# From a router's scores to its first expert: the first block's gather ahead of the extra blocks', accumulators cleared behind the sigmoid, filling products on TensorE

## The chip, the cores and the metric

The kernel runs on one core of a Trainium2 chip. The metric is the device time of one execution in microseconds (us); less is better. A core has five engines that run side by side, each in the order of its own instruction stream: TensorE (PE, matrix products and transposes; PEld is its loading of the stationary operand), VectorE (DVE), ScalarE (ACT), GpSimd (POOL) and SyncE (SP). Here SP issues nearly all weight transfers. POOL issues the transfers that fetch or add rows by index (indirect DMA), and also copies and broadcasts over partitions. They meet through semaphores: an instruction starts when all that it waits for has been signalled.

## What is computed

Two layers of a network over 256 latent and 256 context tokens of 1024 numbers. In each layer a mixer (attention and a linear recurrence) is followed by a mixture of experts, and the change lies between these two, in layer 0 alone, where both kinds of tokens pass through the experts. The router, cut to what matters:

```
scores = sigmoid(h @ router_w)                # 16 experts in 4 groups of 4
biased = scores + router_b
# the group with the largest sum of its two best wins; in it the two best experts
top_w  = scores of the two / their sum
for e in range(16):
    hid = silu(h @ w_gate[e]) * (h @ w_up[e])
    out = out + combine[:, e:e+1] * (hid @ w_down[e])   # combine: top_w, zero if not chosen
x  = x  + g2  * out[latent];  xc = xc + cg2 * out[context]
```

Everything is float32. A token is computed only for the two experts that it chose.

## The kernel before, in words

**Ahead of the router.** Layer 0 ends its mixer in tiles of 128 tokens, four of them. For the last step of each tile and each half h of its columns, `out_turn` (L1134) turns the tile's rows by four transposes (tile names pxa, xaT), and `out_logits` multiplies them with the router's matrix (plog); VectorE then forms the logits lg. `warm(x, n)` puts n products on PE whose result nobody reads; in a float32 product PE's trace has two records for each.

**`route` (L1274).** ScalarE clears two accumulators in PSUM, ccg and ccd (four instructions, L1286 and L1287, by a scale of zero over a constant), which the extra blocks below will use, and takes the sigmoid sc of the logits. In layer 1 there are no such clears, and ten fillers `warm(sc, 10)` stand here. VectorE adds the bias (bi) and finds the winning group and the chosen experts (A, Ab), the normed weights (mb), and PE counts by triangular products the rank of each token in its expert (prank, with Ab as one operand); rk holds it on VectorE. At the end the weight is split into three bfloat16 parts, columns 2 to 4 of `vals` (columns 0 and 1 hold a token's number).

**Slots.** Each expert of layer 0 has one main block of 64 slots and up to three extra blocks of 32; which of these are run is decided on the device by the count (a branch on each engine concerned, `extras`, L1555). `onehot(e)` (L1368) compares the ranks with a row of numbers: four VectorE instructions, one per token tile, each of 512 columns, 128 for each block, into one buffer that all experts share. `infos(e)` (L1378) multiplies it on PE with `vals` (pslot: 16 products of 5 columns, four for each of the four blocks), copies the result (sf), and VectorE gives for each slot the row to fetch (sgs), whether it is of a latent or a context token (sic), and the weight (sw). `gathers(e)` fetches the rows on POOL (xg for the main block, xgx for extra ones); three sets of buffers. `r["counts"]` (L1356) turns the counts into integers for the branches.

**An expert.** `xtranses` turns the rows (pxg to xgT, pxx to xxT); `up_stage` multiplies with the gate and up matrices: `up0` is eight steps of k, each a gate and an up product of 512 columns (a pair, 16 products in all), and `upx` the same for an extra block (32 rows, 256 columns, into ccg). `hid0` and `hidx` form silu(gate) times up (hid, hix; ACT, then DVE). `htranses` and `down_stage` follow (pdn, and ccd for extra blocks). `pick0` and `pickx` choose for each slot the gate g2 or cg2 of the residual, `weigh` multiplies result, weight and gate, and `scatter` adds the rows to the layer's output (yd) by indirect DMA. All matrix products are issued through one helper, so in the profile they share the line L114; they are told apart by their tiles.

`gates2` (L1472) prepares the two gates on POOL, once: four broadcasts of a row over the partitions, each with three copies, and then two subtractions (g2m, g2x) which take the second gate less the first.

**What sets the order.** The whole expert stage is in a manual schedule: PE, POOL, DVE and ACT run exactly in the order in which the Python code is written (from L1630). SP's weight transfers (L216) go to a ring of eight chunks of 2 MB; each waits until the products that read the chunk's former content are done, and from expert 4's on also for an activation of the expert (`mark`), so that the queue stays short. Where written order matters most:

```
onehot(0); infos(0); warm(ident, 8); counts; gathers(0); wd_1 on POOL's queue
onehot(1); infos(1); gathers(1); loads of expert 2
onehot(2); xtranses(0); infos(2); gathers(2); gates2(); onehot(3)
up_stage(0)
infos(3); xtranses(1); gathers(3); onehot(4); htranses(0); up_stage(1); infos(4)
e = 0: down_stage(0); pick0, pickx; weigh, scatter; xtranses(2); gathers(4); onehot(5); infos(5); ...
```

Of the kernel before, what the change touches and what calls it, by code (L numbers as in the profile page):

```python
# [108 lines left out]
def backbone(ctx: ExitStack, tc: tile.TileContext, a: dict):  # L109
# [28 lines left out]
    def ps_tr(name):  # L138
        return psb(name, "tr")
# [326 lines left out]
    def mixer(l, R, hp, hT, mo):  # L466
# [667 lines left out]
        def out_turn(h, t):  # L1134
            pt = ps_tr("pxa")
            for k in range(4):
                pe.transpose(pt[:, k * P:(k + 1) * P], xa[t, h][:, k * P:(k + 1) * P], ident)
            xa[t, h, 1] = hc = t2("xaT")
            act.copy(hc[:], pt)
            if h:  # L1140
                finish(t)
# [132 lines left out]
    def route(l, lg, Q, R):  # L1274
# [8 lines left out]
        cps = {}  # L1283
        for n_ in () if last else ("cg", "cd"):
            t = pp["pool"].tile([P, 1024], F32, name=f"c{n_}", tag=n_, bufs=1)
            act.activation(t[:, 0:512], C("iota"), AF.Copy, scale=0.0)  # L1286
            act.activation(t[:, 512:768], C("iota")[:, 0:256], AF.Copy, scale=0.0)  # L1287
            cps[n_] = t[:, 0:768].rearrange("p (b c) -> p b c", b=3)
        bk.update(cps=cps)
        if last:  # L1290
            warm(sc[:].rearrange("p t e -> p (t e)"), 10)
# [57 lines left out]
        w1 = Q.tile(E16, F32, name="w1")  # L1349
        dve.tensor_copy(vals[:, 0:nt, :, 2], wc[:])  # L1350
        dve.tensor_tensor(w1[:], wc[:], vals[:, 0:nt, :, 2], op=OP.subtract)
        dve.tensor_copy(vals[:, 0:nt, :, 3], w1[:])
        dve.tensor_tensor(w1[:], w1[:], vals[:, 0:nt, :, 3], op=OP.subtract)
        dve.tensor_copy(vals[:, 0:nt, :, 4], w1[:])
# [45 lines left out]

    bk = {}
# [11 lines left out]
    def experts(l, tmp):  # L1413
# [31 lines left out]
        def up0(ps, x, w):  # L1445
            for k in range(8):
                sx = x[:, k % 4, 64 * (k // 4):64 * (k // 4) + 64]
                mm(ps[0:64, :], sx, w[0][:, k, :], k == 0, k == 7)
                mm(ps[64:128, :], sx, w[1][:, k, :], k == 0, k == 7)
# [180 lines left out]
        with tc.manual_schedule(engines=ORDERED):  # L1630
            W[1] = [load_part(l, 1, 0, nc.sync), wx["w"][0][0]]
            wx["i"] += 1
            onehot(0)
            infos(0)
            warm(ident, 8)
            r["counts"](tmp)
            gathers(0)
            W[1].append(load_part(l, 1, 2, nc.gpsimd))
            onehot(1)
            infos(1)  # L1640
            gathers(1)
            W[2] = [load_part(l, 2, i, nc.gpsimd if i < 2 else nc.sync) for i in range(3)]
            onehot(2)
            xtranses(0)
# [4 lines left out]
            up_stage(0)  # L1649
# [375 lines left out]
```

## Time and profile before

| | |
|---|---|
| median of 3 runs | 1109.69 us (1105.55 to 1113.52) |
| the profiled execution, its own time | 1107.49 us |
| its span in the trace | 1105.6 us |
| PE busy | 984.8 us, 89% |
| DVE, ACT, POOL busy | 600.5 (54%), 432.3 (39%), 195.7 (18%) |
| products of expert weights, layer 0 (pdn and both pgu<-..xgT) | 124.3, 118.7, 118.7 us, mean of one 617 to 619 ns |
| HBM traffic | 271 GB/s over the span |

The time of the whole is that of the profiled execution; the span is the trace's own, from its first to its last instruction, 1.9 us less. All places below are times from the span's start. In a row of the timeline stand start, busy time, engine, line, operation, tile written <- tiles read, shape, how many instructions the row gathers, and in brackets how long the engine was idle before and what ended that. The granted clock in a window is 1.00 for 2.4 GHz and 0.50 for 1.2 GHz. In a share of busy time PE's products overlap, so a product's mean is longer than the step from one to the next.

### The profile page before, as it was taken

How to read it: one execution, taken by the hardware profiler on the slowest of the kernel's cores; microseconds unless marked ns; L12 is line 12 of the kernel's file. 1: busy time of each engine (PE TensorE's matmuls, PEld its weight loads, DVE VectorE, ACT ScalarE, POOL GpSimd, SP SyncE). 2: the span in 40 equal slices, each digit the busy share in tenths (PEclk: the TensorE clock that was granted, in tenths of full speed). 3: DMA queues.
4: the chain of work that ended last, by engine and by line, in shares of the span. 5: the costliest groups of instructions: out<-in, count | busy, mean ns of one | idle time of the engine just before them, and what ended most of it. 6: DMA issues, size and time to landing. Idle time of an engine off the chain costs nothing. (4 is left out here: it accounts for less than half of the span.)

```text
span 1105.6 us, 15540 instructions
## 1 busy us (share of the span) xinstructions
PE 984.8 (89%) x5791; PEld 520.2 (47%) x5791; DVE 600.5 (54%) x1363; ACT 432.3 (39%) x858; POOL 195.7 (18%) x208
## 2 busy tenths in 40 slices
PE   5999999899589989999898599897977999999993
PEld 3555465678444434333332366353765434444431
DVE  3567487686743325534433356679863344444445
ACT  3635678465511212212221264796741122221222
POOL 2000033331544313212110200205241000000000
PEclk9999999899669989999998799998997999999996
DMA  9947674011866876999997565558156799999941
GB/s 381 396 167 299 229 272 186 30 39 58 323 244 259 286 287 190 398 407 410 395 397 305 155 268 188 200 180 305 49 210 270 317 421 413 429 400 416 397 197 41
DMA packets 51963, 298.87 MB, mean 270 GB/s; under 512 B 5457, under 2 KB 8401, under 8 KB 35969
## 3 DMA queue, kind: packets, MB, share of 16 engines
q1 hardware_dynamic: 44800, 279.88, 64.1%
q0 software_dynamic: 6896, 16.87, 5.4%
q8 instruction: 73, 1.20, 0.4%
q10 hardware_dynamic: 144, 0.52, 0.1%
q14 instruction: 50, 0.40, 0.1%
HBM read 288.86 MB, written 10.49 MB: 271 GB/s over the span
## 5 line engine op out<-in xcount | busy, mean ns | idle before, releaser
L114 PE MATMUL pdn<-wd,hidT 128*64 128x512 f32 x512 | 124.3, 619 | 5.3 <-PEq L1572 4.0
L114 PE MATMUL pgu<-wg,xgT 128*64 128x512 f32 x256 | 118.7, 617 | 0.3 <-issue 0.3
L114 PE MATMUL pgu<-wu,xgT 128*64 128x512 f32 x256 | 118.7, 617 | 0.2 <-DMA wu<-exp_w_up_dram 0.2
L114 PE MATMUL pgu<-wu,xT 128*64 128x512 f32 x256 | 116.5, 598 | 0.0
L114 PE MATMUL pgu<-wg,xT 128*64 128x512 f32 x256 | 116.5, 598 | 0.0
L1795 DVE SCALAR_TENSOR_TENSOR xtok<-pcb,wc,xtok 128x512 f32<-128x512 f32 x64 | 47.7, 750 | 102.7 <-PE pcb L114 102.7
L1455 DVE TENSOR_TENSOR hid<-hid,pgu 64x512 f32<-64x512 f32 x16 | 11.0, 690 | 126.2 <-ACT hid L1454 126.2
L114 PE MATMUL pproj<-hh,wps 128*128 128x512 f32 x288 | 76.9, 407 | 0.0
L846 POOL TENSOR_TENSOR wo<-wf,wo 128x512 fp32r<-128x512 f32 x29 | 41.0, 1434 | 201.9 <-ACT wo L844 170.1
L1430 POOL DMA_INDIRECT yd<-xtok,sgs x24 | 38.6, 1608 | 185.0 <-DVE xtok L1489 183.5
L114 PEld LDWEIGHTS pdn<-wd,hidT 128*64 128x64 f32 x512 | 34.7, 140 | 67.5 <-issue 66.8
L114 PEld LDWEIGHTS pgu<-wg,xgT 128*64 128x64 f32 x256 | 34.8, 142 | 65.2 <-issue 64.7
L114 PEld LDWEIGHTS pproj<-hh,wps 128*128 128x128 f32 x288 | 53.2, 188 | 19.6 <-issue 6.5
L114 PEld LDWEIGHTS pgu<-wg,xT 128*64 128x64 f32 x256 | 32.5, 136 | 61.6 <-issue 60.7
L1454 ACT ACTIVATE hid<-pgu 64x512 f32<-64x512 f32 x16 | 9.4, 590 | 104.8 <-PE pgu L114 104.7
L1954 POOL TENSOR_TENSOR fin<-xtok,fin 128x512 f32<-128x512 f32 x2 | 2.5, 1278 | 254.8 <-DVE xtok L1795 254.8
L1748 ACT ACTIVATE hid<-pgu 64x512 f32<-64x512 f32 x16 | 9.4, 589 | 94.6 <-PE pgu L114 94.5
L795 ACT ACTIVATE Pm<-psc,mx,qy 128x512 f32<-128x512 f32 (+1 forms) x48 | 33.5, 703 | 21.3 <-DVE mx L789 21.1
L497 DVE TENSOR_TENSOR wps<-win,wps 128x512 fp32r<-128x512 f32 x48 | 32.6, 687 | 14.9 <-ACT wps L496 14.4
L114 PE MATMUL pproj<-hT,wps 128*128 128x512 f32 x144 | 39.8, 397 | 0.0
L114 PEld LDWEIGHTS pgu<-wu,xgT 128*64 128x64 f32 x256 | 34.8, 142 | 6.9 <-issue 5.2
L114 PE MATMUL pwa<-wo,mh 128*128 128x512 f32 x128 | 36.3, 407 | 1.6 <-POOL wo L846 0.9
(442 smaller groups left out, 2079.5 us busy)
## 6 DMA issues: line engine op xcount, KB each, us to landing
wd<-exp_w_down_dram SPq DMA_DIRECT2D x31, 2048.0 KB, 14.2
wu<-exp_w_up_dram SPq DMA_DIRECT2D x27, 2048.0 KB, 9.6
wg<-exp_w_gate_dram SPq DMA_DIRECT2D x27, 2048.0 KB, 15.9
xtok<-ada_w_dram SPq DMA_DIRECT2D x7, 2048.0 KB, 7.4
win<-w_in_dram SPq DMA_DIRECT2D x6, 2048.0 KB, 16.2
adac<-ada_w_dram SPq DMA_DIRECT2D x5, 2048.0 KB, 8.0
xtok<-ada_w_dram SPq DMA_DIRECT2D x8, 1024.0 KB, 5.1
adac<-ada_w_dram SPq DMA_DIRECT2D x8, 1024.0 KB, 4.9
```

Source lines behind the costliest of these rows:

```text
L114: pe.matmul(out, lhsT, rhs, start=start, stop=stop)
L497: dve.tensor_tensor(wl, wv, wh.bitcast(F32), op=OP.subtract)
L795: act.activation(ps[h], sc_[i][h], AF.Exp, bias=mx[:, h:h + 1], scale=qr[:, ti, j, h:h + 1], accum_out=sm[:, h:h + 1])
L846: pool.tensor_tensor(lo, w, hi.bitcast(F32), op=OP.subtract)
L1430: st = pool.indirect_dma_start(out=dst, out_offset=bass.IndirectOffsetOnAxis(ap=idx, axis=0), in_=y, in_offset=None, bounds_check=dst.shap ...
L1454: mark.append(act.activation(sg, ps[0:64, :], AF.Silu).ins.name)
L1455: dve.tensor_tensor(h.rearrange("s k p -> s (k p)"), sg, ps[64:128, :], op=OP.mult)
L1748: act.activation(sg, ps[0:64, :], AF.Silu)
L1795: dve.scalar_tensor_tensor(x, cb, wc[:, t, e:e + 1], x, op0=OP.mult, op1=OP.add)
L1954: (dve if q else pool).tensor_tensor(fin["t"][:, 1 + t, cs], x, fin["t"][:, 0, cs], op=OP.mult)
```

## The change: what it does

All of it is in layer 0. (a) `out_turn` puts seven fillers ahead of each half of the last tile's transposes. (b) In `route` the sigmoid comes first; the clears read the sigmoid (times zero) and so stand behind it on ScalarE. Twenty fillers stand on PE ahead of the ranks; layer 1 keeps its ten. (c) The three weight parts of `vals` are made later, by `parts`, from a copy of the weights. (d) A generator `first_info` takes the place of `onehot(0)` and `infos(0)`: first the one-hot columns and the slot products (columns 0 and 1 of `vals`) of the main block alone and its gather; then those of the extra blocks, the counts and their gathers; the weight columns come at the third call, on PE between the two halves of expert 0's `up0`. (e) The order from there: expert 0's first half of `up0` follows `onehot(1)`; `infos(1)`, `gathers(1)`, the loads of expert 2, the transposes of the extra blocks and `onehot(2)` come between the halves; `infos(2)`, `gathers(2)`, `gates2` and `onehot(3)` follow `up0`, the extra products and the hidden products instead of preceding them. The program's own generator resumes at each `next(fi)`.

```diff
@@ -1132,6 +1132,8 @@
                 nc.sync.dma_start(tokens(yd[l])[t], xtok[:, t, :])
         def out_turn(h, t):
+            if not last and t == tiles[-1]:
+                warm(ident, 7)
             pt = ps_tr("pxa")
             for k in range(4):
                 pe.transpose(pt[:, k * P:(k + 1) * P], xa[t, h][:, k * P:(k + 1) * P], ident)
@@ -1281,14 +1283,16 @@
         sc = Q.tile(E16, F32, name="sc")
         act.activation(sc[:], lg[:], AF.Sigmoid)
         cps = {}
+        n_t = nt * NE
         for n_ in () if last else ("cg", "cd"):
             t = pp["pool"].tile([P, 1024], F32, name=f"c{n_}", tag=n_, bufs=1)
-            act.activation(t[:, 0:512], C("iota"), AF.Copy, scale=0.0)
-            act.activation(t[:, 512:768], C("iota")[:, 0:256], AF.Copy, scale=0.0)
+
+            z = sc[:].rearrange("p t e -> p (t e)").unsqueeze(1)
+            act.activation(t[:, 0:512].rearrange("p (i c) -> p i c", c=n_t), z.broadcast_to([P, 512 // n_t, n_t]), AF.Copy, scale=0.0)
+            act.activation(t[:, 512:768].rearrange("p (i c) -> p i c", c=n_t), z.broadcast_to([P, 256 // n_t, n_t]), AF.Copy, scale=0.0)
             cps[n_] = t[:, 0:768].rearrange("p (b c) -> p b c", b=3)
         bk.update(cps=cps)
-        if last:
-            warm(sc[:].rearrange("p t e -> p (t e)"), 10)
+        warm(sc[:].rearrange("p t e -> p (t e)"), 10 if last else 20)
         bi = Q.tile(E16, F32, name="bi")
         dve.tensor_tensor(bi[:], sc[:], vec[:, VRB:VRB + NE].unsqueeze(1).broadcast_to(E16), op=OP.add)
@@ -1346,12 +1350,19 @@
         rt_all[l] = dict(rk=rk, ci=ci, oi=oi, nt=nt, n=n, nx=nx, wc=wc, counts=lambda tmp: counts(l, tmp, cnt, ci, oi))
         if last:
             return
-        w1 = Q.tile(E16, F32, name="w1")
-        dve.tensor_copy(vals[:, 0:nt, :, 2], wc[:])
-        dve.tensor_tensor(w1[:], wc[:], vals[:, 0:nt, :, 2], op=OP.subtract)
-        dve.tensor_copy(vals[:, 0:nt, :, 3], w1[:])
-        dve.tensor_tensor(w1[:], w1[:], vals[:, 0:nt, :, 3], op=OP.subtract)
-        dve.tensor_copy(vals[:, 0:nt, :, 4], w1[:])
+        wcr = R.tile(E16, F32, name="wcr", tag="lg", bufs=1)
+        dve.tensor_copy(wcr[:], wc[:])
+
+        def parts(tmp):
+
+            w1 = tmp.tile(E16, F32, name="w1")
+            dve.tensor_copy(vals[:, 0:nt, :, 2], wcr[:])
+            dve.tensor_tensor(w1[:], wcr[:], vals[:, 0:nt, :, 2], op=OP.subtract)
+            dve.tensor_copy(vals[:, 0:nt, :, 3], w1[:])
+            dve.tensor_tensor(w1[:], w1[:], vals[:, 0:nt, :, 3], op=OP.subtract)
+            dve.tensor_copy(vals[:, 0:nt, :, 4], w1[:])
+
+        rt_all[l]["parts"] = parts
     def counts(l, tmp, cnt, ci, oi):
@@ -1398,6 +1409,41 @@
         dve.tensor_reduce(w[:], f[:, :, 2:5], axis=AX.X, op=OP.add)
         return gs, w, ic
+    def first_info(l, tmp, nx, rbase):
+
+        nt = rt_all[l]["n"] // P
+        nb = 1 + nx
+        oh = tmp.tile([P, nt, nb * P], BF16, name="oh", tag=f"oh{nb}", bufs=1)
+        f = tmp.tile([P, nb, 5], F32, name="sf", tag=f"sf{nb}", bufs=2)
+        g = tmp.tile([P, nb], F32, name="sg_", tag=f"sg_{nb}", bufs=2)
+        gs = tmp.tile([P, nb], I32, name="sgs", tag=f"sgs{nb}", bufs=12)
+        ic = tmp.tile([P, nb], F32, name="sic", tag=f"sic{nb}", bufs=12)
+        w = tmp.tile([P, nb], F32, name="sw", tag=f"sw{nb}", bufs=12)
+
+        def take(bs, cs):
+            pt = ps_tr("pslot")
+            for b in bs:
+                for t in range(nt):
+                    mm(pt[:, b * 5 + cs.start:b * 5 + cs.stop], oh[:, t, b * P:(b + 1) * P], vals[:, t, 0, cs], t == 0, t == nt - 1)
+            act.copy(f[:, bs.start:bs.stop, cs], pt[:, 0:5 * nb].rearrange("p (b c) -> p b c", c=5)[:, bs.start:bs.stop, cs])
+
+        for bs in (range(0, 1), range(1, nb)):
+            b = slice(bs.start, bs.stop)
+            for t in range(nt):
+                c = slice(P * bs.start, P * bs.stop)
+                dve.tensor_scalar(oh[:, t, c], C("iota")[:, c], rbase[:, t:t + 1], None, op0=OP.is_equal)
+            take(bs, slice(0, 2))
+            dve.tensor_tensor(g[:, b], f[:, b, 0], f[:, b, 1], op=OP.add)
+            if b.start:
+                dve.tensor_scalar(gs[:, b], g[:, b], 2.0, C("half")[:, 1:2], op0=OP.mult, op1=OP.add)
+            else:
+                dve.tensor_scalar(gs[:, b], g[:, b], C("half")[:, 0:1], None, op0=OP.add)
+            yield gs, w, ic
+        dve.tensor_scalar(ic[:], g[:], 2.0 * S - 65536, None, op0=OP.is_lt)
+        take(range(nb), slice(2, 5))
+        dve.tensor_reduce(w[:], f[:, :, 2:5], axis=AX.X, op=OP.add)
+        yield
+
     bk = {}
     def blocks(l, tmp):
@@ -1442,8 +1488,8 @@
             act.copy(o[:], pt.rearrange("p (k s) -> p k s", k=4))
             return o
-        def up0(ps, x, w):
-            for k in range(8):
+        def up0(ps, x, w, ks=range(8)):
+            for k in ks:
                 sx = x[:, k % 4, 64 * (k // 4):64 * (k // 4) + 64]
                 mm(ps[0:64, :], sx, w[0][:, k, :], k == 0, k == 7)
                 mm(ps[64:128, :], sx, w[1][:, k, :], k == 0, k == 7)
@@ -1630,23 +1676,34 @@
         with tc.manual_schedule(engines=ORDERED):
             W[1] = [load_part(l, 1, 0, nc.sync), wx["w"][0][0]]
             wx["i"] += 1
-            onehot(0)
-            infos(0)
+            fi = first_info(l, tmp, nx, rk[:, :, 0])
+            info[0] = next(fi)
+            gs0 = info[0][0]
+            gather(gs0[:, 0:1], xg0[0], h2d[l][:])
             warm(ident, 8)
+            next(fi)
             r["counts"](tmp)
-            gathers(0)
+            extras(Pe, 0, lambda b: gather(gs0[:, 1 + b:2 + b], xgx[b][0], h2x))
             W[1].append(load_part(l, 1, 2, nc.gpsimd))
+            r["parts"](tmp)
             onehot(1)
+            x0 = xtrans0(xg0[0])
+            ps = psb("pgu", "mm")
+            up0(ps, x0, W[0], range(4))
+            next(fi)
             infos(1)
             gathers(1)
             W[2] = [load_part(l, 2, i, nc.gpsimd if i < 2 else nc.sync) for i in range(3)]
+            xt[0] = x0, xtransx(0)
             onehot(2)
-            xtranses(0)
+            skip_hint(f"up{l}_0", 0)
+            up0(ps, x0, W[0], range(4, 8))
+            extras(PEe, 0, lambda b: upx(b, xt[0][1], W[0]), f"up{l}_0")
+            hid[0] = hid0(ps), hidx()
             infos(2)
             gathers(2)
             gates2()
             onehot(3)
-            up_stage(0)
             infos(3)
             xtranses(1)
             gathers(3)
```

How this moves instructions, at the places that the next parts speak of. The rows are an engine's instructions in program order: line, operation, tile written <- tiles read with the tile's own number, shape, and how many in a row.

PE, from the last tile's transposes to the ranks, difference (- before, + after; one filler is one row's count):

```order
-L1137 MATMUL pxa<-ident,xa 128x128 x8
+L114 MATMUL warm<-ident 128x128 x3
+L1139 MATMUL pxa<-ident,xa 128x128 x4
+L114 MATMUL warm<-ident 128x128 x7
+L1139 MATMUL pxa<-ident,xa 128x128 x4
 L114 MATMUL plog<-vec,xaT 128x16 x8
+L114 MATMUL warm<-ident,sc 64x128 x20
 L114 LDWEIGHTS tri
```

The last seven fillers stand directly ahead of the second half's transposes, and the twenty read sc, so they begin when the sigmoid is there.

DVE around expert 0's hidden products, before (oh_2823 and oh_2917 are the one-hots of experts 2 and 3, sgs_2866 the slot numbers of expert 2, hid_3051 and hix_3054 expert 0's hidden products, sg__3076 the begin of expert 3's slot numbers):

```order
L1375 TENSOR_SCALAR oh_2823<-cst_64,rk_2654 128x512 x4
L1392 TENSOR_TENSOR sg__2865<-sf_2863 128x4
L1394 TENSOR_SCALAR sic_2867<-sg__2865 128x4
L1395 TENSOR_SCALAR sgs_2866<-sg__2865,cst_64 128x1
L1397 TENSOR_SCALAR sgs_2866<-sg__2865,cst_64 128x3
L1398 TENSOR_REDUCE sw_2868<-sf_2863 128x4
L1375 TENSOR_SCALAR oh_2917<-cst_64,rk_2654 128x512 x4
L1572 UNCONDITIONAL_BRANCH x2
L1455 TENSOR_TENSOR hid_3051<-hid_3051,pgu_2922 64x512
L1526 TENSOR_TENSOR hix_3054<-hix_3054,ccg_2604 64x768
L1392 TENSOR_TENSOR sg__3076<-sf_3074 128x4
```

And after (hid_3039 and hix_3042 are expert 0's hidden products, sgs_3065 expert 2's slot numbers, oh_3116 expert 3's one-hots, sg__3140 the begin of expert 3's slot numbers):

```order
L1501 TENSOR_TENSOR hid_3039<-hid_3039,pgu_2815 64x512
L1572 TENSOR_TENSOR hix_3042<-hix_3042,ccg_2620 64x768
L1403 TENSOR_TENSOR sg__3064<-sf_3062 128x4
L1405 TENSOR_SCALAR sic_3066<-sg__3064 128x4
L1406 TENSOR_SCALAR sgs_3065<-sg__3064,cst_64 128x1
L1408 TENSOR_SCALAR sgs_3065<-sg__3064,cst_64 128x3
L1409 TENSOR_REDUCE sw_3067<-sf_3062 128x4
L1386 TENSOR_SCALAR oh_3116<-cst_64,rk_2691 128x512 x4
L1403 TENSOR_TENSOR sg__3140<-sf_3138 128x4
```

Expert 2's slot numbers and expert 3's one-hots, which stood ahead of expert 0's hidden products, now stand behind both.

POOL, the last gather of expert 2 and the begin of the gates, after (the first ISA row of L1524 changes POOL's configuration, the second is the first broadcast):

```order
L1471 DMA xgx2_2_2602<-h2d0_1248,sgs_3065 128x256
L1618 UNCONDITIONAL_BRANCH
L1524 ISA
L1524 ISA xtok_65<-adas02_1221 128x512
L1618 UNCONDITIONAL_BRANCH
L1525 COPY g2m_2703<-xtok_65 64x512
L1527 COPY g2x_2704<-xtok_65 32x256 x2
```

The order on POOL itself is as before, but the gathers ahead of the gates read sgs_3065, the slot numbers that have moved.

## Rows read from the trace of the kernel before

**Rows 1.** Waits of SP's queue, 285 to 630 us: total, times, longest.

```profile
SPq L216 <- ACT hid L1454: 101.2, 8, 22.7
```

**Rows 2.** The same view, all engines: PE for expert weights.

```profile
PE pgu L114 <- DMA wu<-exp_w_up_dram: 0.2, 1, 0.2
```

**Rows 3.** Windows: length, busy us (instructions) per engine, granted TensorE clock, DMA share, GB/s.

```profile
286.00:288.00 2.00, 0.64 (x3) 0.67 (x4) 2.00 (x6) 1.41 (x3) 0.58 (x1) 0.50 0.99 408
320.00:322.00 2.00, 2.00 (x8) 0.68 (x6) 0.17 (x1) 0.00 (x0) 1.09 (x1) 0.50 1.02 414
834.00:836.00 2.00, 2.00 (x12) 1.64 (x11) 1.76 (x10) 0.00 (x0) 0.00 (x0) 0.50 0.65 131
```

**Rows 4.** Timeline, layer 0's router scores: start, length, engine, operation [idle before, releaser].

```profile
295.99 0.23 DVE L1151 SCALAR_TENSOR_TENSOR lg<-plog,n2y,lg 128x16 f32<-128x16 f32 x1
297.62 0.24 ACT L1282 ACTIVATE sc<-lg 128x64 f32<-128x64 f32 x1
```

**Rows 5.** Timeline, PE ahead of and at layer 0's ranks.

```profile
290.80 1.09 PE L1137 MATMUL pxa<-ident,xa 128*128 128x128 f32 x4 [2.36 <-DVE xa L1128]
302.94 0.22 PE L114 MATMUL prank<-Ab,tri 128*128 128x16 bf16 x2 [7.26 <-DVE bi L1325]
```

**Rows 6.** Timeline, PE: layer 1's ten filling products (two records each).

```profile
832.36 4.47 PE L114 MATMUL warm<-ident,sc 128*32 128x128 f32 x20 [0.86 <-ACT sc L1282]
```

**Rows 7.** Timeline, from the gathers to the first expert; layer 1's small one-hots last.

```profile
308.44 1.14 POOL L1425 DMA_INDIRECT xg<-h2d,sgs  x1 [5.61 <-DVE gt L1359]
310.67 1.20 POOL L1425 DMA_INDIRECT xgx<-h2d,sgs  x1 [1.10 <-DVE oh L1375]
312.19 1.09 PE L1440 MATMUL pxg<-ident,xg 128*128 128x128 f32 x4 [0.62 <-DMA xg<-h2d,sgs]
317.47 1.12 PE L114 MATMUL pgu<-wg,xgT 128*64 128x512 f32 x1
837.77 0.73 DVE L1723 TENSOR_SCALAR ohf<-cst,rk 128x64 f32<-128x64 f32 x4
```

**Rows 8.** Timeline, PE: expert products at half clock, full clock, behind a pause.

```profile
320.09 1.06 PE L114 MATMUL pgu<-wg,xgT 128*64 128x512 f32 x1
320.94 1.06 PE L114 MATMUL pgu<-wg,xgT 128*64 128x512 f32 x1
352.55 3.65 PE L114 MATMUL pdn<-wd,hidT 128*64 128x512 f32 x16
409.67 6.12 PE L114 MATMUL pdn<-wd,hidT 128*64 128x512 f32 x16
```

**Rows 9.** Timeline, behind the extra blocks' last products of expert 0.

```profile
337.47 0.57 PE L114 MATMUL pslot<-vals,oh 128*128 128x5 bf16 x16
338.47 0.96 DVE L1526 TENSOR_TENSOR hix<-hix,ccg 64x768 f32<-64x768 f32 x1 [8.72 <-ACT hix L1525]
340.19 0.30 DVE L1397 TENSOR_SCALAR sgs<-sg__3076,cst 128x3 int32<-128x3 f32 x1
```

**Rows 10.** Timeline, POOL: last gather of expert 2, then the gates.

```profile
323.83 1.03 POOL L1425 DMA_INDIRECT xgx<-h2d,sgs  x1 [2.74 <-DMA wd<-exp_w_down_dram]
336.29 0.81 POOL L1478 PARTITION_BROADCAST xtok<-adas  x1 [11.43 <-DMA xgx<-h2d,sgs]
345.37 0.85 POOL L1481 COPY g2x<-xtok 32x256 f32<-32x256 f32 x2
355.01 1.27 POOL L1483 TENSOR_TENSOR g2m<-g2m 128x512 f32<-128x512 f32 x1 [8.79 <-DVE sw L1398]
```

**Rows 11.** Timeline, POOL: a broadcast behind two-input operations, elsewhere.

```profile
189.22 1.79 POOL L347 PARTITION_BROADCAST a2b<-adax  x2 [5.91 <-ACT mh L1215]
```

**Rows 12.** Timeline, expert 0's weighting and expert 5's slots.

```profile
356.31 1.21 DVE L1486 SCALAR_TENSOR_TENSOR xtok<-g2m,sic 128x512 f32<-128x512 f32 x1 [2.14 <-POOL g2m L1483]
362.77 1.67 DVE L1375 TENSOR_SCALAR oh<-cst,rk 128x512 bf16<-128x512 f32 x4
364.50 0.48 PE L114 MATMUL pslot<-vals,oh 128*128 128x5 bf16 x13 [0.22 <-DVE oh L1375]
```


## The prediction, made before the changed kernel was run

> **What bounds the kernel now.** I read the page's busy shares first: TensorE (PE) works 89% of the span, everything else at most 54%. The question is therefore where PE pauses, and whether a pause at layer 0's first expert can be made up later. The waits answer the second half: from 285 to 630 us SP's weight loads stand behind the experts' own work, one line of it 101.2 us [rows 1], while PE's products wait 0.2 us for expert weights [rows 2]. The loads follow PE, so what PE loses or gains at expert 0 moves all that follows. The windows give the clock: 0.50 at 286 and at 320 [rows 3]. The timeline gives the stretch itself: the last router scores at 295.99, the sigmoid only at 297.62 [rows 4], ranks at 302.94 behind a pause of 7.26 [rows 5], gather at 308.44, first transposes 312.19, first expert product 317.47 [rows 7], and the next slots at 337.47, which I call T [rows 9]. I call the same place T' in the changed kernel.
>
> **Part 1: the scores come earlier.** Scores end at 295.99 + 0.23 = 296.22, and the sigmoid starts 1.40 later because four clears of the accumulators precede it on ScalarE. They now stand behind it and delay nothing until expert 0's extra products, 30 us later: gain 1.3. The 14 fillers ahead of the last tile's transposes cost at most 14 x 0.22 = 3.1 at half clock (one filler is two records; layer 1's ten are 20 records in 4.47, so 0.22 a record at a granted 0.50 [rows 3, 6], 0.45 a filler, 6.3 for 14); but the second seven lie in a pause of 2.36 before the row at 290.80 [rows 5], the first behind work already queued. By the two ends, 0 and 0.8, I take +0.4: sigmoid done at 296.95.
>
> **Part 2: twenty fillers ahead of the ranks.** At half clock they take 20 x 0.447 = 8.9, at full clock half of that, 4.5. The ranks cannot start before the choice of experts is done: that took 302.94 - 297.86 = 5.1 behind the sigmoid [rows 4, 5]. So the ranks start between 302.0 and 305.9, against 302.94. Layer 1's fillers stayed at 0.50 throughout [rows 3]; the first expert's products changed to full clock only between 320.9 and 327 [rows 8]. I take 7.0, between the ends: ranks at 304.0, +1.1. Without the fillers it would be 302.0.
>
> **Part 3: the first gather.** Ranks to gather took 5.50 [rows 5, 7]. Now only 128 of 512 one-hot columns stand ahead: four of 512 take 1.67 [rows 12], four of 64 take 0.73 [rows 7], so about 0.85 for 128, -0.8. Sixteen slot products take 0.57 [rows 9], four about 0.15, -0.4. The five weight parts, which lay among the one-hots, leave: a short VectorE operation takes 0.23 [rows 4], say 0.2 each, -1.0. That makes 3.3 and the gather 307.3, 1.1 early. Landing takes 312.19 - 308.44 = 3.75 [rows 7]; transposes (1.09) and copy add 1.8: first product at 312.9, 4.6 early (bounds 2.7 and 6.7).
>
> **Part 4: the first products in two halves.** Between the halves stand sixteen slot products (0.57), then expert 1's slots and expert 0's extra transposes (0.95). Expert 1's one-hots use the one buffer that these slot products read, so VectorE begins them only then: 1.67 plus the handing over, 2.3. Together 3.8, of which 2.3 is an empty PE. A pair of products takes 0.85 at half clock (320.09 to 320.94) and 3.65 / 8 = 0.46 at full [rows 8], so one half of eight pairs costs 6.8 or 3.6. I take 6.0 for the first (most of it at half) and 4.6 for the second: behind a pause of 3.46 the down products took 6.12 instead of 3.65 [rows 8]. 312.9 + 6.0 + 3.8 + 4.6 = 327.3, against 327.0 (T, 337.5, less the extra products' 10.5). So T' = T + 0.3; all bounds one way give T - 5.6, the other T + 5.2. The head start is spent on work that used to stand ahead of the first product.
>
> **Part 5: what now stands behind the up products.** Expert 2's slots, its gathers, the gates and expert 3's one-hots used to precede the up stage and now follow it. On VectorE, expert 2's slot numbers come behind the extra hidden product, which ended at T + 2.0 (338.47 + 0.96 [rows 9]); slot numbers at T' + 2.6, then expert 3's one-hots, 1.7. PE waits for these before expert 1's transposes: T' + 4.6 instead of T + 0.4, **+4.2**.
>
> POOL works in order. Expert 2's gathers need the slot numbers: T' + 3.3, the last one 2.2 later (308.44 to 310.67 [rows 7]), done at T' + 6.7 = 344.5. Then the gates. Before, 11.43 passed between the last gather and the first broadcast, and 8.79 between the last copy and the two-input operation [rows 10]. The first broadcast waits for the gathers' landing, to which the profile puts the 11.43; the two-input operation reads only POOL's own copies. Ahead of both the program has POOL change its set of functions, and the pause recurs where a broadcast follows two-input operations elsewhere, 5.91 [rows 11]. For the first I take 9.0 (ends 5.91, the change alone, and 11.43, the landing as before, when the transfers were full: DMA share 1.02 [rows 3]), for the second 8.79. From first broadcast to last copy took 336.29 to 346.22, 9.93 [rows 10]. Sum: 344.5 + 9.0 + 9.9 + 8.8 + 1.3 (the operation) = 373.5, against 356.28: the gates are **17.2** late. Before, this long chain was covered by expert 0's up products.
>
> Who waits: VectorE's pick for expert 0 already waited 2.14 for the gates [rows 12], and behind it in VectorE's order stand expert 0's weighting and expert 5's one-hots, for which PE's slots at 364.50 wait. Picks 2.43, weighting 0.75 + 1.27, one-hots 1.67, last slots 0.2 make 6.3 [rows 12]: slots end at 379.8 instead of 364.98, **+14.8**. PE itself would arrive at 364.5 + 0.3 + 4.2 = 369.0, so it stands some 10 us, and the 4.2 is inside the 14.8. Such a pause drops the clock: 6.12 - 3.65 = **+2.5** [rows 8].
>
> The Trainium skill ("GPSIMD Engine Reference", section 2.1 Instruction dispatch) says that the first call into a freshly loaded function on this engine pays an instruction load of about 6 us, 5.95 measured. The 5.91 of [rows 11] agrees; 8.79 and 11.43 of [rows 10] are longer. With the page's figure twice the gates would come 5.9 earlier, and the time would be about 1119.
>
> **Sum.** +14.8 + 2.5 = +17.3 on the profiled execution's 1107.5: 1124.8. The median of the runs, 1109.69, lies 2.2 above that execution; I forecast 1126, between the sums on either. Within this case all favourable ends (T - 5.6, both changes 5.91, no clock loss) give +3.0, 1110.5; all unfavourable (T + 5.2, 11.43, 8.79) give 337.5 + 5.2 + 6.7 + 11.4 + 9.9 + 8.8 + 1.3 + 6.3 = 387.1, +22.1 + 2.5, 1132.
>
> **Rivals.** *First: the gates are not on the path.* The profile puts the 11.43 to a gather's landing [rows 10]. If both pauses of POOL are waits for others' work, and later do not occur, the gates finish at 344.5 + 9.9 + 1.3 = 355.7, no later than before. Then the later transposes remain: +0.3 + 4.2 = +4.5, 1112 (bounds 1106 and 1117). Against it: 8.79 passes between POOL's own operations with nothing landing.
>
> *Second, not slower: PE is at full clock from the router on.* The fillers keep PE busy where it paused 7.26 [rows 5]; if the clock rises within them and stays, the ranks start at 302.0 and both halves cost 3.6. With the gates as in the first rival the time is -5.6 + 4.2 = -1.4, 1106. It decides from a head start of 4.2 on. Against it: the same filling work stayed at 0.50 in layer 1 [rows 3, 6], and PE is empty again during the gather's 3.75.
>
> The Trainium skill ("TensorE: Matmul & The Clock Gate", section What's actually happening) says that throttled is the default and that activity releases it, which would favour this rival. The row of layer 1's fillers did not show it; no row here shows twenty.
>
> **How the numbers follow.** Chances: main case 0.75, first rival 0.17, second 0.08. The forecast is the main case's. 1109 to 1132 holds nearly all of the main case and about two thirds of the first rival. About 1%, 11 us, is what a measurement of this kernel can tell from no change: 1120.8 and up is slower. Roughly 0.72 of the main case lies there, 0.54. Faster by over 1% would need 1098.6, which no case reaches; I keep 0.03 for what I have missed. The rest, 0.43, is within 1%.
>
> **What would show it.** Right: sigmoid near 296.5; ranks near 304; first expert product near 313; an empty PE of about 2 between the halves; expert 0's last extra products ending near 338; POOL's two-input operation of the gates near 372, with a pause of 6 to 9 before it and another before the first broadcast; VectorE's pick waiting for it over 10 us; PE's slots for expert 5 waiting about as long and ending near 380; half clock behind. Wrong: gates done before 360 (first rival), clock 1.00 in the fillers and both halves (second), or a shift at 380 that shrinks by 617, where the experts end: then PE was not what the later experts waited for.

## The result, and the profile after

The changed kernel takes 1138.45 us (median of 4 runs, 1135.67 to 1139.34) against 1107.93 for the kernel before beside it: a ratio of 1.0275, 95% interval 1.0245 to 1.0305. It is slower, as forecast, but by about 30 us where some 17 were forecast, and outside the range.

The page after:

```profile
span 1137.0 us, 15719 instructions
...
PE 999.3 (88%) x5875; PEld 531.3 (47%) x5875; DVE 605.5 (53%) x1369; ACT 432.0 (38%) x860; POOL 192.9 (17%) x208
...
q8 instruction: 80, 1.31, 0.5%
...
L114 PE MATMUL pdn<-wd,hidT 128*64 128x512 f32 x512 | 125.6, 615 | 12.0 <-PEq L1618 7.3
```

Two of these rows on the page before:

```profile
q8 instruction: 73, 1.20, 0.4%
...
L114 PE MATMUL pdn<-wd,hidT 128*64 128x512 f32 x512 | 124.3, 619 | 5.3 <-PEq L1572 4.0
```

PE has 84 products more (5875 against 5791) and as many weight loads: 168 instructions. The queue q8 carries instructions, in packets of 16 KB: 80 with 1.31 MB, where before there were 73. In layer 1 of the kernel before, from 670 to 1075 us, the trace has on the average 254 instructions of PE (products, weight loads, branches) between two of them, so q8 is read here as PE's own code. The 168 instructions added are less than one such packet, so most of the seven packets more are not the added code itself. The row of the down products counts both layers (256 records each, also in the table of the kernel before). PE's idle time ahead of them has more than doubled, 12.0 us against 5.3, and 7.3 of it (4.0 before) is put to PE's own sequencer, not to another engine.

The timeline of ScalarE and of PE at the router and expert 0 (columns as in [rows 4]):

```profile
296.56 0.24 ACT L1284 ACTIVATE sc<-lg 128x64 f32<-128x64 f32 x1
```

```profile
296.86 7.27 PE L114 MATMUL warm<-ident,sc 128*64 128x128 f32 x40 [2.12 <-ACT sc L1284]
304.07 0.21 PE L114 MATMUL prank<-Ab,tri 128*128 128x16 bf16 x2
...
312.50 1.01 PE L114 MATMUL pgu<-wg,xgT 128*64 128x512 f32 x1 [0.68 <-ACT xgT L1488]
...
318.92 0.18 PE L114 MATMUL pslot<-vals,oh 128*128 128x5 bf16 x1 [0.58 <-DVE oh L1386]
...
321.24 0.64 PE L114 MATMUL pgu<-wg,xgT 128*64 128x512 f32 x1
```

The sigmoid has moved from 297.62 to 296.56, the ranks from 302.94 to 304.07, the first expert product from 317.47 to 312.50 [rows 4, 5, 7]. Between the halves PE pauses for expert 1's one-hots, four times, 1.2 us in sum, and the second half starts at 321.24.

POOL at the gates, VectorE's pick, and PE behind expert 0's extra products:

```profile
340.07 1.02 POOL L1471 DMA_INDIRECT xgx<-h2d,sgs  x1 [0.30 <-issue]
350.42 0.80 POOL L1524 PARTITION_BROADCAST xtok<-adas  x1 [9.33 <-DMA xgx<-h2d,sgs]
...
367.50 1.25 POOL L1529 TENSOR_TENSOR g2m<-g2m 128x512 f32<-128x512 f32 x1 [7.76 <-issue]
```

```profile
368.79 1.21 DVE L1532 SCALAR_TENSOR_TENSOR xtok<-g2m,sic 128x512 f32<-128x512 f32 x1 [9.75 <-POOL g2m L1529]
```

```profile
335.33 0.55 PE L114 MATMUL pslot<-vals,oh 128*128 128x5 bf16 x16
338.51 0.18 PE L114 MATMUL pslot<-vals,oh 128*128 128x5 bf16 x1 [2.62 <-DVE oh L1386]
...
373.59 0.18 PE L114 MATMUL pslot<-vals,oh 128*128 128x5 bf16 x1 [5.86 <-DVE oh L1386]
...
378.94 1.09 PE L1486 MATMUL pxg<-ident,xg 128*128 128x128 f32 x4 [2.38 <-DMA xg<-h2d,sgs]
```

These answer [rows 9, 10, 12]: the gates' operation starts at 367.50 instead of 355.01, the pick waits 9.75 instead of 2.14, and PE's slots for expert 5 wait 5.86 ahead of the first product, where before only the 0.22 between the later ones is shown. The last row is new: expert 3's gather stands behind the gates on POOL, and PE waits 2.38 for it.

So far this is the forecast's mechanism. It does not make 30 us. The following table tells where the rest came in: the start of each expert's main silu (ScalarE, hid) less that in the kernel before, in us.

| expert | 0 | 1 | 2 | 4 | 6 | 8 | 11 | 14 | layer 1, last |
|---|---|---|---|---|---|---|---|---|---|
| kernel before, start | 328.4 | 348.0 | 376.2 | 427.9 | 461.7 | 491.5 | 541.7 | 586.0 | 1074.1 |
| changed kernel | -2.1 | +4.5 | +14.0 | +6.7 | +9.1 | +19.8 | +31.2 | +39.6 | +31.9 |
| after_pad44 | -2.4 | +4.8 | +14.5 | +15.4 | +15.4 | +15.4 | +15.8 | +16.6 | +13.7 |
| before_pad84 | +0.6 | +1.3 | +3.7 | -2.5 | +0.9 | +10.4 | +25.8 | +34.2 | +25.6 |
| gates_back | +3.6 | +3.6 | +6.5 | +0.2 | +6.8 | +16.4 | +28.5 | +37.1 | +33.2 |
| gates_back_pad44 | +2.7 | +2.7 | +5.9 | +7.1 | +7.2 | +7.2 | +7.3 | +9.0 | +6.3 |

The four kernels below the changed one are those of the experiments. Each row is one profiled execution; that of gates_back, 1141.1 us, is the longest of its five and 9.5 above their median.

In the changed kernel the shift is 14.0 at expert 2, falls to 6.7 at expert 4 and then grows to 39.6, where nothing was edited. PE's pauses there, in a stretch of 40 us (releaser "PEq" is PE's sequencer, "issue" nothing that the profile shows):

```profile
465.02 0.59 PE L114 MATMUL pgu<-wu,xgT 128*64 128x512 f32 x1 [1.22 <-issue]
472.85 0.58 PE L114 MATMUL pslot<-vals,oh 128*128 128x5 bf16 x16 [2.09 <-PEq L1618]
...
485.32 0.59 PE L114 MATMUL pgu<-wg,xgT 128*64 128x512 f32 x1 [1.69 <-issue]
493.39 0.55 PE L114 MATMUL pslot<-vals,oh 128*128 128x5 bf16 x16 [1.84 <-PEq L1618]
499.30 1.07 PE L114 MATMUL pdn<-wd,hidT 128*64 128x512 f32 x2 [1.78 <-issue]
```

Some lie in the middle of a run of products that all read one chunk of weights which has already landed. Beside them, from the trace's DMA packets, the start of the last 16 KB packet on the instruction queue, and how long after this packet's end the pause ends:

```
pause begins  length  instruction packet starts  pause ends after packet's end
470.76        2.09    470.19                     1.71
483.64        1.69    482.94                     1.34
491.55        1.84    490.79                     1.64
497.52        1.78    497.06                     1.28
552.73        1.64    552.00                     1.42
```

The last column is nearly constant, and not in these five alone. Taken from 317.5 us to layer 0's last down product, the sixteen traces of this case have 115 pauses of PE over 1 us; 90 of them end 1.2 to 2.0 us after the end of a q8 packet, and none 2.0 to 2.7 us after it. Spread evenly, only about one in ten would. In the kernel before it is all four (8.5 us in sum), in the changed kernel 11 of 14 (22.6 us); the three others are the 2.62, 5.86 and 2.38 above, waits for one-hots and for a gather. One of the 11, 3.40 us from 558.99, the profile puts to a weight transfer, but the products behind it are transposes, which read no weights; the products of the experts' weights wait for no transfer in this stretch.

Below, the sum of PE's pauses over 0.25 us is taken over the same stretch; a pause is counted "at a fetch" when an instruction packet starts less than 1.5 us before it or within it, and ends within it. Before: 22.9 us, 6.5 of it at fetches. After: 48.8, 24.0 at fetches; of these the 2.62 at 338.51 is the wait for one-hots above, which falls together with a fetch. These sums go by coincidence in time and by one execution each, so a microsecond or two of them is uncertain. Behind some of the pauses the granted clock falls too (windows of the changed kernel, columns as in [rows 3]):

```profile
470.00:480.00 10.00, 6.99 (x43) 2.47 (x41) 5.55 (x14) 1.57 (x3) 1.38 (x2) 0.83 1.03 423
490.00:500.00 10.00, 6.38 (x39) 2.04 (x35) 4.15 (x11) 1.56 (x3) 0.00 (x0) 1.00 0.80 308
560.00:570.00 10.00, 7.62 (x22) 2.43 (x24) 0.00 (x0) 0.37 (x1) 0.71 (x1) 0.66 0.97 360
```

It is 0.83 behind the pause at 470.76 and 0.66 behind the 3.40 at 558.99, but 1.00 around the two pauses between 490 and 500. The Trainium skill ("Runtime: NRT & Kernel Launch", section Instruction fetch mechanics) says that each engine's instructions come in blocks of 16 KiB, 256 instructions, that a crossing is mostly hidden, and that a taken branch to a block not at hand costs a fetch. The packets here have that size, and the 254 instructions between two of them in layer 1 agree with 256; that crossings are hidden is not what these rows show.

### The profile page after: what moved, and what is told of

Same layout as the page of the kernel before. It is cut to its first block, busy times and chain, and to the rows that moved or that the text cites. A ratio compares the mean times of both kernels' runs of the same rounds, so it can differ in the third digit from the quotient of the medians.

```text
span 1137.0 us, 15719 instructions
## 1 busy us (share of the span) xinstructions
PE 999.3 (88%) x5875; PEld 531.3 (47%) x5875; DVE 605.5 (53%) x1369; ACT 432.0 (38%) x860; POOL 192.9 (17%) x208
## 3 DMA queue, kind: packets, MB, share of 16 engines
q8 instruction: 80, 1.31, 0.5%
## 5 line engine op out<-in xcount | busy, mean ns | idle before, releaser
L114 PE MATMUL pgu<-wg,xgT 128*64 128x512 f32 x256 | 121.5, 627 | 3.0 <-issue 2.3
L114 PE MATMUL pgu<-wu,xgT 128*64 128x512 f32 x256 | 121.4, 626 | 1.9 <-issue 1.9
L795 ACT ACTIVATE Pm<-psc,mx,qy 128x512 f32<-128x512 f32 (+1 forms) x48 | 33.5, 702 | 22.3 <-DVE mx L789 22.2
```

Source lines behind the costliest of these rows:

```text
L114: pe.matmul(out, lhsT, rhs, start=start, stop=stop)
L795: act.activation(ps[h], sc_[i][h], AF.Exp, bias=mx[:, h:h + 1], scale=qr[:, ti, j, h:h + 1], accum_out=sm[:, h:h + 1])
```

## The experiments

"Small product" below is a bfloat16 product of 16 columns put at the very start of the program, where PE is idle for 10 us; each is two PE instructions, and nobody reads its result. It moves all later PE code. Each ratio of this section is to runs of the kernel before on the same chip, whose median was 1106.36 to 1112.2 us from chip to chip, so the ranges in us of the expectations can be read to about half a per cent.

```diff
         if l == 0:
+            pw = ps_tr("warm")
+            for _ in range(44):
+                mm(pw[0:16, 0:16], onesb[:, 0:16], onesb[:, 0:16], True, True)
             for s in range(2):
```

**The place of the code alone, in both kernels.**

> The changed kernel with 44 small bfloat16 products (16 columns, 88 PE instructions) put at the very start, where PE is idle for its first 10 us. Every PE instruction behind the router then stands 168 + 88 = 256 instructions later than in the kernel before. Theory A (the pauses that PE shows from expert 6 on are waits for its own instructions, and where they fall depends on where a 16 KB piece of 256 instructions begins): the pauses that lie at a fetch, 24.0 us in the changed kernel against 6.5 before, go back towards 6.5, the gates' delay stays: 1113 to 1123 us. Theory B (the weights' transfers lost their lead behind the late gates, and PE waits for weights): the place of the instructions is nothing, 1136 to 1141 us.

Measured: 1121.27 us, ratio 1.0087 (1.0053 to 1.0122); pauses at fetches 8.9 us. Adding 44 products took the changed kernel's ratio from 1.0275 to 1.0087, 1.9% or about 20 us. The table of shifts shows where: what grew from expert 6 on is gone, the shift stays between 15 and 17.

> The kernel before with 84 of the same small products at the start: 168 PE instructions, so that all behind the router stands where it does in the changed kernel, with none of the change's work. Theory A: pauses at fetches from expert 6 on as in the changed kernel, 1118 to 1132 us. Theory B: 1105 to 1111 us, as before.

Measured: 1133.1 us, 1.1 above theory A's range, ratio 1.0179 (1.0141 to 1.0217); pauses at fetches 22.3 us, in the same kinds of place:

```profile
457.26 0.64 PE L114 MATMUL pgu<-wg,xgT 128*64 128x512 f32 x1 [1.54 <-issue]
465.21 0.57 PE L114 MATMUL pslot<-vals,oh 128*128 128x5 bf16 x16 [2.58 <-PEq L1575]
...
490.32 1.02 PE L114 MATMUL pdn<-wd,hidT 128*64 128x512 f32 x2 [1.22 <-issue]
```

None of the change's work is in this kernel. Theory A stands in both directions; theory B (weights late) falls: it gave 1136 to 1141 us for after_pad44 and 1105 to 1111 for this kernel.

> Control. The kernel before with 128 of the small products at the start: 256 PE instructions, one whole 16 KB piece, so that all behind stands again as in the kernel before. Theory A (where a piece of 256 begins decides): as the kernel before, within 4 us of it, pauses at fetches about 6.5 us. Rival C (any number of added instructions costs, through more fetching or through the products themselves): more than the 84 products cost, 1130 us or above.

Measured: 1110.07, ratio 0.9992 (0.9970 to 1.0014); pauses at fetches 8.4. More products than before_pad84, and no loss: rival C falls, and the cost repeats with 256 instructions.

> The kernel before with 32 small products (64 PE instructions) at the start: another place for the 16 KB pieces, a quarter of a piece on. Theory A: pauses at fetches lie between those of the kernel before (6.5 us) and of the one with 168 instructions (22.3), or outside on either side, and the time goes with them one to one: 1100 to 1135 us; the sum of pauses in the trace tells which. If a number of added instructions below one piece cost in proportion, it would be 1107 + 21 x 64 / 168 = 1115 us.

> The same with 64 small products, 128 instructions, half a piece on. Theory A: 1100 to 1135 us, with the sum of PE's pauses. In proportion: 1123 us.

> The same with 108 small products, 216 instructions, 40 short of a whole piece. Theory A: 1100 to 1135 us, nearer to the kernel before than with 168 if cost rises and falls with the distance from it. In proportion: 1134 us.

Measured, with the others by instructions added to the kernel before:

| added | 0 | 64 | 128 | 168 | 216 | 256 |
|---|---|---|---|---|---|---|
| ratio | 1 | 0.9949 | 1.0115 | 1.0179 | 1.0147 | 0.9992 |
| 95% interval | | 0.9929, 0.9969 | 1.0071, 1.0160 | 1.0141, 1.0217 | 1.0111, 1.0183 | 0.9970, 1.0014 |
| pauses at fetches, us | 6.5 | 1.1 | 23.0 | 22.3 | 21.5 | 8.4 |
| pauses over 1 us that end 1.2 to 2.0 us after a packet's end, us | 8.5 | 1.1 | 25.5 | 27.3 | 20.4 | 9.7 |
| packets on q8 (page) | 73 | 71 | 78 | 80 | 76 | 74 |

The medians of the three are 1101.06, 1120.76 and 1123.47 us. The time is not in proportion to what was added: 64, 216 and 256 instructions contradict that. It follows the pauses, roughly one to one. Whether 216 is better than 168, the intervals don't tell. The worst place and the best lie 2.3% of the time apart, 25 us, nearly three times the 0.8% that the late gates cost below. The count of packets follows the place too, in all sixteen runs: 73 or 74 at the old place, 71 or 72 at the place of 64, 80 at that of 168, whether the change's work is in the kernel or not.

**The gates.** The four lines go back ahead of the second half of expert 0's up products:

```diff
             onehot(2)
+            infos(2)
+            gathers(2)
+            gates2()
+            onehot(3)
             skip_hint(f"up{l}_0", 0)
...
             hid[0] = hid0(ps), hidx()
-            infos(2)
-            gathers(2)
-            gates2()
-            onehot(3)
```

> The changed kernel with expert 2's slots and gathers, the gates and expert 3's one-hots put back ahead of the up products, between the two halves of expert 0's. The instruction count ahead of expert 1 is as in the changed kernel. Both theories: the pick for expert 0 no longer waits 9.75 us for the gates, and the pauses of 2.62, 5.86 and 2.38 us around the slots of experts 3 and 5 go. Theory A: the later pauses stay, 1124 to 1131 us. Theory B: with the gates early the transfers keep their lead and the later pauses go too: 1103 to 1110 us.

Measured: 1131.57, ratio 1.0167 (1.0132 to 1.0203). The pick waits 2.27 instead of 9.75:

```profile
360.06 1.22 DVE L1532 SCALAR_TENSOR_TENSOR xtok<-g2m,sic 128x512 f32<-128x512 f32 x1 [2.27 <-POOL g2m L1529]
```

The waits of 2.62, 5.86 and 2.38 are gone as well, but the shift still grows from 6.5 at expert 2 to 37.1 at expert 14: theory A, though 0.6 us above its range.

> Both edits: the gates ahead of the up products and 88 small instructions at the start. Theory A: neither the gates' delay nor the later pauses are left, and the head start at expert 0 (2 us) remains: 1101 to 1109 us. Theory B: the same as with the gates alone.

Measured: 1112.61, ratio 1.0007 (0.9979 to 1.0034), 3.6 us above what theory A gave. Against after_pad44 on the same chip this is 1.0087 - 1.0007 = 0.8%, 9 us for the late gates; against gates_back, also on this chip, 1.0167 - 1.0007 = 1.6%, 18 us for the place. No head start is left: the silu of expert 0 comes 2.7 later than before, since the waits for one-hots between the halves are followed by half clock: the second half takes 6.5 us (323.26 to 329.74) instead of the 3.7 of the changed kernel (321.24 to 324.90).

```profile
324.00:328.00 4.00, 4.00 (x12) 1.19 (x10) 2.23 (x9) 0.01 (x1) 2.81 (x5) 0.50 0.81 252
```

And of after_pad44, with the gates late:

```profile
367.64 0.41 PE L1559 MATMUL pxx<-ident,xgx 128*128 128x128 f32 x2 [0.28 <-issue]
374.47 0.19 PE L114 MATMUL pslot<-vals,oh 128*128 128x5 bf16 x1 [6.42 <-DVE oh L1389]
...
379.57 1.09 PE L1489 MATMUL pxg<-ident,xg 128*128 128x128 f32 x4 [1.96 <-DMA xg<-h2d,sgs]
```

With the code in its old place the gates' own wait is 6.42, and the gather behind them 1.96. Its shift then stays at 15.4 from expert 4 to 8, 13.7 at the end: that is the price of the forecast's mechanism by itself, in one profiled execution.

**Parts of the first gather.** The first expert's one-hots move to a part of another tile, xtok:

```diff
-        oh = tmp.tile([P, nt, nb * P], BF16, name="oh", tag=f"oh{nb}", bufs=1)
+        oh = xtok[:].rearrange("p t d -> p (t d)")[:, 2560:3584].bitcast(BF16).rearrange("p (t c) -> p t c", t=nt)
```

> The changed kernel with the gates back ahead of the up products, 88 small instructions at the start, and the first expert's one-hots in a buffer of their own, so that expert 1's one-hots need not wait for the slot products between the two halves. If the pause between the halves (2.3 us) and the half clock behind it are what spends the head start of 5.0 us at the first product (312.43 against 317.47): the last extra product of expert 0 ends at 335 to 338 instead of 340.2 and the time is 3 to 6 us under that of the same kernel with one buffer. Rival: expert 2's one-hots then wait for the buffer instead and the pause only moves: 0 to 2 us.

Measured: 1109.7, ratio 0.9998 (0.9973 to 1.0024). Expert 0's last extra product ends at 334.2 (its sigmoid lay 1.5 us early in this execution). The pause moves, as the rival has it (0.64 for expert 2's one-hots), but the second half runs at full clock again, and from expert 4 to expert 14 the shift is between -0.1 and +1.1, where gates_back_pad44 has +7.1 to +9.0. The times don't show this: 0.9998 against 1.0007 is 1 us, with intervals that overlap, as the rival gave. The execution traced here is the fastest of its ten, 3.7 us under their median, so what the buffer is worth stays open.

> As the kernel with a buffer of its own, and expert 2's slots, gathers, the gates and expert 3's one-hots between the second half of expert 0's up products and its extra products, so that PE's second half waits for nothing of expert 2. If PE's pauses between the halves matter: last extra product at 334 to 336, 2 to 3 us before that of the kernel before, and the time 4 to 8 us under that of the kernel with the gates between the halves and one buffer. If the gates, now a little later on POOL, end the wait instead: the pick for expert 0 waits for them and the gain is lost by expert 2.

Measured: 1109.64, ratio 0.9985 (0.9960 to 1.0011). The last extra product ended at 334.0 as expected, but the pick waits 4.90 for the gates; at expert 2 the shift was -1.1, at expert 4 already +2.5, in an execution 4.0 us above the median. By the ratio it is 2 us under gates_back_pad44, not the 4 to 8 expected, and the intervals overlap: no gain is shown.

> The changed kernel without its twenty fillers ahead of the ranks, with 84 small products at the start, so that the instruction places are those of the changed kernel with 44. If the fillers matter for the clock: ranks at 302 to 303.6 instead of 304.1, but slots, transposes and the first products at half clock, the last extra product 1 to 3 us later, the time 1 to 4 us over that of the changed kernel with 44 small products. If only their length matters: 0.5 to 2 us under it.

Measured: 1127.57, ratio 1.0136 (1.0075 to 1.0197): 5 us over after_pad44 where 1 to 4 were expected, though the intervals overlap; the ranks came at 305.25, not at 302 to 303.6. From sigmoid to expert 0's silu it takes 32.4 us without the fillers (298.20 to 330.64) and 29.5 with them in after_pad44 (296.48 to 326.01): the twenty fillers are worth 2.9 us there, in one execution each. The sigmoid itself is 1.7 later, which arose ahead of the router, where the 84 products also move the code.

**Do the costs add, and which kernel is best?**

> The kernel before with 32 small products again, on the same chip as the two above: ratio 0.993 to 0.997, against which the changed order at the same place is read.

> The changed kernel as it is, its instructions at the same place (76 small products). If place and late gates simply add: 1.0087 less 0.005, ratio 1.001 to 1.006; the pauses at fetches behind expert 2 as few as in the kernel before with 32, and expert 2's shift still about 14 us. If the late gates cost less or more at another place: outside.

> The changed kernel with the gates ahead of the up products, the first one-hots in a buffer of their own, and 76 small products, so that all behind the router stands 320 = 256 + 64 PE instructions later than in the kernel before: the place that was best in the scan. If the two repairs and the place add: 1.000 less 0.005, ratio 0.993 to 0.997, some 6 us under the kernel before. If the head start of the changed order, hidden so far behind the next wait, shows at this place: below 0.993.

Measured on one chip: before_pad32b 1102.34, ratio 0.9916 (0.9884 to 0.9948); after_pad76 1116.5, 1.0056 (1.0034 to 1.0077), pauses at fetches 1.1; own_buffer_pad76 1103.89, 0.9936 (0.9916 to 0.9956). The kernel before with 32 lies a little under its range, the two others within theirs. So place and repairs add about as forecast, but only to the width of the intervals: the place alone gave 0.8% in the kernel before, 0.6% with the two repairs and 0.3% in the changed kernel as it is. In the trace of after_pad76 expert 2's shift is 21.4, not about 14: its sigmoid came 3.1 us later than in after_pad44; from expert 4 on the shift is 15 to 17. At the best place the changed order with its two repairs is no better than the old order, whose 32 products compute nothing; between these two no difference is shown.

## Why the prediction was wrong

**Parts 1 to 3 held by number.** Sigmoid 296.56 (forecast done at 296.95, so begun at 296.7), fillers 7.27 (7.0), ranks 304.07 (304.0), first product 312.50 (312.9). For part 1 this was in part luck:

```profile
294.67 2.09 ACT L1112 ACTIVATE h<-xa,n2y 128x512 f32<-128x512 f32 x2 [1.45 <-DVE n2y L369]
```

The scores were done at 295.28 (VectorE's last lg), 0.9 earlier than before and not 0.4 later, since the last tile's transposes ran at a granted clock of 1.00 (286 to 294 us) where it had been 0.50. The sigmoid did not follow them: it stood behind ScalarE's own work on h, which ended at 296.76. The sum in part 1 is also wrong as written: fourteen fillers of two records at half clock are the 6.3 of its bracket, not at most 3.1. In part 2 the 7.0 was a choice between two ends, not worked out; it fitted because the clock rose within the fillers, from 0.50 until 302 us to 0.90 from 302 to 304.

**Part 4 was too dear.** The second half ran at full clock, 3.6 instead of 4.6, the first took 5.3 instead of 6.0, and PE stood 1.2 between them instead of 2.3: T' is 335.3, T - 2.1, where T + 0.3 was taken; inside the bounds (of which the lower one, added up again, is T - 5.2, not T - 5.6).

**Part 5 held in kind.** Expert 1's transposes come at T' + 4.7 (4.6). POOL's pauses were 9.33 and 7.76 (9.0 and 8.79); the gates' operation started at 367.5 (372), the slots for expert 5 ended at 375.3 (379.8), +10.3 instead of +14.8. Not in the sum was expert 3's gather behind the gates, 2.38. With the clock behind it (granted 0.53 from 370 to 380 us) the shift is 14.0 at expert 2, and 15 to 17 for the later experts where the code has its old place. The rivals fell: the gates ended at 368.75, not before 360; the clock was 0.50 again in most of the first half, and no head start outlived expert 0.

**What failed is the step from there to the end:** "what PE loses or gains at expert 0 moves all that follows", with nothing added. The change adds 168 PE instructions, and the sum counted their time alone. They also move each later instruction against the 16 KB pieces in which PE's code is fetched, and in these experts that costs 1.0275 - 1.0087 = 1.9%, about 20 us (with the gates put back, 1.6%, 18 us). The prediction had no term for it. By the ratio the forecast's mechanism alone is worth 0.9%, 10 us (13.7 in the profiled execution), for which 17.3 were summed. The kernel before showed it too: the pause of 3.46 which I used as a price for the clock [rows 8] lies at a fetch (packet at 406.91, pause from 405.96 to 409.42), and I did not ask what had caused it:

```profile
409.42 0.32 PE L114 MATMUL pslot<-vals,oh 128*128 128x5 bf16 x6 [3.46 <-issue]
```

That same pause and its half clock, 3.46 + 2.5 us, are missing in the changed kernel; they are some 6 of the 7.3 us by which its shift fell from expert 2 to 6.7 at expert 4.

## What to carry to other kernels

When a change adds or removes instructions ahead of a long stretch of branching code on the busiest engine, its time can move by more than the edit is worth; put a few cheap instructions at an idle place, in two or three numbers, before judging the edit. A shift that grows where nothing was edited need not be a late buffer: look at pauses that the profile puts to the engine's own sequencer or to nothing, and lay the instruction packets beside them. Here the page alone gave a first sign, the number of packets on the instruction queue, 80 against 73. And an order that is moved off one wait needs the next one named: here gates, one-hots and gathers on in-order engines took back 5 us of head start before expert 1.

## What was not expected of the hardware

PE's pauses at fetches of its own code take up to 4.3 us each (after_pad44, 420.79) in a stretch where the DMA share is near 1.0, and in the kernel before they come to between 1.1 and 23.0 us in this stage, by the place alone. Why one place pauses and another does not stays open, and so does what passes in the 1.2 to 2.0 us between a packet's end and PE's next product. Some pauses follow the branch over blocks that are not run (472.85, 493.39), as the Trainium skill's rule on branches would have it, others stand in the middle of a run of products (485.32, 499.30), and no run here changed the branches or the load of the DMA queues.
